# One input and one output matrix per group in the S5 scan of a decoder layer, on one core

## The chip, the cores and the metric

The kernel runs on one core of a Trainium2 chip. A core has TensorE (PE, matrix products into PSUM), VectorE (DVE), ScalarE (ACT), GpSimd (POOL) and SyncE (SP, which here issues most DMA transfers); each works through its own instructions in order and waits on semaphores for the others. The metric is the device time of one execution in microseconds (us); lower is better. The time before is the median of three executions.

## The reference

The program is one decoder layer for 1024 tokens of width 1024: half a SwiGLU block, a mixing stage (native sparse attention beside an S5 diagonal state space), the other half block, a final norm. The change touches the S5 part alone:

```python
dt = exp(log_dt); mag = exp(lr * dt)
ab_re, ab_im = mag * cos(li * dt), mag * sin(li * dt)
bu = einsum('btgh,gph->btgp', u, bb)          # complex, bb = f * b; 32 groups, 16 channels, 64 states
x[t] = ab * x[t-1] + bu[t]                    # complex, as an associative scan over 1024 tokens
y = einsum('btgp,ghp->btgh', xr, c_re) - einsum('btgp,ghp->btgh', xi, c_im) + d_skip * u
y = gelu(y); s = y * sigmoid(y @ w_glu + b_glu)
```

## The kernel before

The stages follow each other: first FFN (`gate_up7`, then `down`), input projection (`project`) with the S5 units and the compression of keys and values beside it, attention, GLU and output projection, second FFN. Most matrix products are made of three products of split operands (`mm3`, L118 to L120). S5 uses plain f32 products.

**How S5 is tiled.** 1024 tokens are 128 chunks of 8. A tile has 128 partitions: 64 states, real part in partitions 0 to 63, imaginary part in 64 to 127. In a chunk the recurrence is unrolled into matrices, so that 8 x 16 inputs of a group give the chunk's contribution to the state, and the state before the chunk gives 8 x 16 outputs. Across the 128 chunks the complex factor of a step is a length, `rho`, and an angle. The kernel turns every chunk's contribution back by the angle so far (multiplication by cosines and sines), so a real scan with `rho` does the recurrence, and turns the result forth again.

**Tables.** `s5_params` (in `gate_up7`, in the first FFN) works out what depends on the parameters and keeps it in DRAM. `s5_tables` makes the matrices in batches of four groups: four batches in the first FFN's `gate_up7`, four in its `down`. Per batch there are four tables, each of three DVE operations (helper `table`, L703 to L709); two of them (the input matrices, `s5t[0]` and `s5t[1]`) are then transposed on PE (L716), copied by ACT (L718) and stored (L719), the other two (the output matrices, `s5t[2]` and `s5t[3]`) are stored as they are (L722, L735). `s5t[4]` holds the matrices inside a chunk. `s5_phases` works out cosines and sines of 128 chunks on POOL, beside `down`, and stores them as `s5t[5]` and `s5t[6]`.

**Units.** `s5_units` has eight units of four groups, each with three steps between which the projections go on: seven loads of 256 KB on SP's queue (L804); then four matmuls with the first input matrix (L809) and four with the second (L811), DVE's two multiplications by cosines and sines (L813, L814), addition (L815), a copy that spreads `rho` into `dk` (L816), the scan (L818) and two multiplications (L819, L820) into `cz` and `sz`; then for each of four groups three matmuls into one PSUM tile, inside the chunk (L824), with `cz` (L825) and with `sz` (L826), a copy by ACT (L828) and stores (L830). Tiles with `bufs=2` are double-buffered: of the seven loads the first two, and no other.

**What sets the order.** The code is one Python program that is unrolled when it is built. A framework puts each engine's instructions in an order at build time, by priority (mostly the order of the code) and by when its own estimates have an instruction ready; it adds the waits, and a tile's buffer is only given again when its last user is done. `s5_units`, `s5_tables` and `s5_phases` are generators: the surrounding stage calls the next step at fixed places (`until`, `self.step`). The tables' steps have a lower priority than the FFN around them.

Of the kernel before, what the change touches and what calls it, by code (L numbers as in the profile page):

```python
# [9 lines left out]
F32 = mybir.dt.float32  # L10
# [3 lines left out]
AF = mybir.ActivationFunctionType  # L14
OP = mybir.AluOpType
# [4 lines left out]
P = 128  # L20
# [102 lines left out]
class Kern:  # L123
# [530 lines left out]
    def s5_tables(self, pool, b0, b1, out):  # L654
# [26 lines left out]
        for g0 in range(b0 * B, b1 * B, B):  # L681
# [18 lines left out]
            def table(x, y, zr, zi, sub, n, name):  # L700
# [7 lines left out]
                TE.tensor_tensor(o[:, :, :n], o[:, :, :n], q[:, :, :n], op=OP.subtract if sub else OP.add)  # L708
                return o  # L709

            for dst, x, y, zx, zy, sub in ((0, bp, bq, rr, ri, False), (1, bp, bq, ri, rr, True)):
                o = table(x, y, zx, zy, sub, 8, "tw")
                yield
                p = self.ps.tile([P, B, P], F32, tag="tr", name="tr", bufs=2)
                for i in range(B):
                    nc.tensor.transpose(p[:, i, :], o[:, i, :8, :].rearrange("p j h -> p (j h)"), self.ident)  # L716
                gt = pool.tile([P, B, P], F32, tag="gt", name="gt", bufs=1)
                nc.scalar.activation(gt, p, AF.Copy)  # L718
                out.dma_start(self.s5t[dst][:, gs, :], gt)  # L719
                yield  # L720
            o = table(cp, cq, ar, ai, False, 9, "tw")
            out.dma_start(self.s5t[2][:, gs, :], o[:, :, 1:9, :].rearrange("p g j h -> p g (j h)"))  # L722
# [11 lines left out]
            o = table(cq, cp, ar, ai, True, 9, "tw")  # L734
            out.dma_start(self.s5t[3][:, gs, :], o[:, :, 1:9, :].rearrange("p g j h -> p g (j h)"))  # L735
# [3 lines left out]
        for j in range(8 * (b1 == 8)):  # L739
            nc.sync.dma_start(self.s5t[4][j * 16:j * 16 + 16], self.s5k[:, :, (7 - j) * 16:(7 - j) * 16 + P])  # L740
            yield

    def s5_phases(self, pool):

        CE, B, NG, L = self.nc.gpsimd, 4, 32, 4
        pw = pool.tile([P, 14 * NG], F32, name="pw")
        CE.dma_start(pw, self.s5keep[:, self.s5keep.shape[1] - 14 * NG:])
        cw, sw = (pw[:, i * 7 * NG:(i + 1) * 7 * NG].rearrange("p (k g) -> p k g", g=NG) for i in range(2))
# [21 lines left out]
        for g0 in range(0, NG, B):  # L770
# [7 lines left out]
            CE.dma_start(self.s5t[5][:, gs, :], ct)  # L778
            CE.dma_start(self.s5t[6][:, gs, :], st)
# [3 lines left out]
    def s5_units(self, pool):  # L783
        nc, v = self.nc, self.nc.vector
        B = 4
        rho = pool.tile([P, 32], F32, name="rho")
        nc.sync.dma_start(rho, self.s5rho)
        cz, sz = (pool.tile([P, B, P], F32, name=f"z{i}") for i in range(2))
        dk = pool.tile([P, B, P], F32, name="dk")
        for t in (cz, sz, dk):  # L790
            nc.gpsimd.memset(t[:, :, 0:1], 0.0)
        for un in range(8):
# [14 lines left out]
            p0, p1 = (self.ps.tile([P, B, P], F32, tag="tr", name="tr", bufs=2) for _ in range(2))  # L807
            for i in range(B):
                nc.tensor.matmul(p0[:, i, :], tb[0][:, i, :], ut[:, uo + i, :], start=True, stop=True)  # L809
            for i in range(B):  # L810
                nc.tensor.matmul(p1[:, i, :], tb[1][:, i, :], ut[:, uo + i, :], start=True, stop=True)  # L811
            a1, a2 = (pool.tile([P, B, P], F32, tag=f"sa{i}", name=f"sa{i}", bufs=1) for i in range(2))
            v.tensor_mul(a1, p0, tb[5])  # L813
            v.tensor_mul(a2, p1, tb[6])  # L814
            v.tensor_add(a1, a1, a2)  # L815
            v.tensor_copy(dk[:, :, 1:], rho[:, gs].unsqueeze(2).to_broadcast([P, B, P - 1]))  # L816
            f = lambda t: t.rearrange("p g c -> p (g c)")
            v.tensor_tensor_scan(f(a2), f(dk), f(a1), 0.0, op0=OP.mult, op1=OP.add)  # L818
            v.tensor_mul(cz[:, :, 1:], a2[:, :, :P - 1], tb[5][:, :, :P - 1])  # L819
            v.tensor_mul(sz[:, :, 1:], a2[:, :, :P - 1], tb[6][:, :, :P - 1])  # L820
# [843 lines left out]
```

## Time and profile before

| what | value |
|---|---|
| time of three executions, us | 2045.43, 2039.56, 2040.13 (median 2040.13) |
| the profiled execution, us | 2044.72, its span 2042.9 |
| mean granted TensorE clock | 0.984 |
| busy share of the span | PE 96%, DVE 66%, ACT 41%, POOL 20% |
| loads of S5 tables (L804) | 56 of 256 KB |
| S5 tables made | about 250 to 640 us |
| S5 units on PE | 781.9 to 938.4 us |

Times in the trace are microseconds from the start of the span. A row of a timeline gives start, length, engine, line, operation, output and inputs, and in brackets how long the engine had been idle and what ended that. Matmuls are pipelined: a row's length is longer than the distance from one start to the next. Lines are those of the kernel's file; the changed file has other numbers for the same code (L809 becomes L812, L824 becomes L830, L825 becomes L831).

### The profile page before, as it was taken

How to read it: one execution, taken by the hardware profiler on the slowest of the kernel's cores; microseconds unless marked ns; L12 is line 12 of the kernel's file. 1: busy time of each engine (PE TensorE's matmuls, PEld its weight loads, DVE VectorE, ACT ScalarE, POOL GpSimd, SP SyncE). 2: the span in 40 equal slices, each digit the busy share in tenths (PEclk: the TensorE clock that was granted, in tenths of full speed). 3: DMA queues.
4: the chain of work that ended last, by engine and by line, in shares of the span. 5: the costliest groups of instructions: out<-in, count | busy, mean ns of one | idle time of the engine just before them, and what ended most of it. 6: DMA issues, size and time to landing. Idle time of an engine off the chain costs nothing.

```text
span 2042.9 us, 26293 instructions
## 1 busy us (share of the span) xinstructions
PE 1951.3 (96%) x9240; PEld 1597.8 (78%) x9240; DVE 1354.2 (66%) x2610; ACT 844.6 (41%) x1609; POOL 403.2 (20%) x552
## 2 busy tenths in 40 slices
PE   6899999999999999889899998898999999999998
PEld 5678788778877888878778887776788888888886
DVE  7768866876696462375689888767765555544546
ACT  7423333342132242143788778564233333322223
POOL 1101100114881001021565663321000000000000
PEclk9999999999999999989899999898999999999999
DMA  6343333437355354652000003653442322262312
GB/s 237 124 147 109 103 94 84 124 120 260 116 182 168 101 181 142 189 167 78 1 22 12 17 16 114 201 198 127 140 130 87 93 73 82 87 217 80 122 57 104
DMA packets 149494, 240.24 MB, mean 118 GB/s; under 512 B 18352, under 2 KB 84160, under 8 KB 149232
## 3 DMA queue, kind: packets, MB, share of 16 engines
q1 hardware_dynamic: 146112, 227.74, 35.4%
q0 software_dynamic: 3248, 10.80, 1.5%
q8 instruction: 73, 1.20, 0.2%
q14 instruction: 61, 0.50, 0.1%
HBM read 172.10 MB, written 68.49 MB: 118 GB/s over the span
## 4 chain that ended last, share of the span: by engine, by line
PE 42%; DVE 4%; POOL 2%; DMA 2%; ACT 2%; issue 2%; SPq 0%; DVEq 0%; ACTq 0%; POOLq 0%
PE dn L120 4%; PE dn L119 4%; PE dn L118 4%; PE mA L118 4%; PE mA L119 4%; PE mA L120 3%; PE pt L1053 2%; PE mB L119 2%; PE mB L120 2%; PE mB L118 2%; POOL e L1031 1%; PE s L1018 1%; PE po L1045 1%; PE po L1046 1%; PE s L1019 1%
## 5 line engine op out<-in xcount | busy, mean ns | idle before, releaser
L118 PE MATMUL mA<-f,wu 128*128 128x512 f32 x584 | 231.9, 398 | 15.5 <-DVE t L357 6.5
L457 DVE SCALAR_TENSOR_TENSOR x<-dn,x 128x512 f32<-128x512 f32 x192 | 130.6, 686 | 165.1 <-PE dn L120 151.3
L119 PE MATMUL mA<-f,wu 128*128 128x512 f32 x584 | 230.1, 394 | 0.0
L120 PE MATMUL mA<-f,wu 128*128 128x512 f32 x584 | 230.0, 394 | 0.0
L307 ACT ACTIVATE wu<-wraw 128x512 fp32r<-128x512 f32 x220 | 137.5, 629 | 188.8 <-PE mA L120 74.3
L431 ACT ACTIVATE a<-ra 128x512 fp32r<-128x512 f32 (+1 forms) x96 | 57.2, 595 | 315.8 <-PE dn L119 304.1
L308 DVE TENSOR_TENSOR wu<-wraw,wu 128x512 fp32r<-128x512 f32 x220 | 150.4, 687 | 50.1 <-ACT wu L307 48.3
L118 PE MATMUL dn<-whi,a 128*128 128x512 f32 x384 | 150.7, 392 | 0.1
L120 PE MATMUL dn<-whi,a 128*128 128x512 f32 x384 | 150.2, 392 | 0.3 <-DVE a L432 0.3
L119 PE MATMUL dn<-wlo,a 128*128 128x512 f32 x384 | 150.0, 391 | 0.0
L118 PEld LDWEIGHTS mA<-f,wu 128*128 128x128 f32 x584 | 110.1, 189 | 48.0 <-DVE t L357 10.7
L1031 POOL TENSOR_TENSOR e<-e,l 128x640 f32<-128x640 f32 (+7 forms) x128 | 132.6, 1067 | 2.5
L120 PEld LDWEIGHTS mA<-f,wu 128*128 128x128 f32 x584 | 110.2, 189 | 24.4 <-issue 0.8
L119 PEld LDWEIGHTS mA<-f,wu 128*128 128x128 f32 x584 | 110.2, 189 | 23.1 <-issue 0.6
L120 PE MATMUL dn<-f,a 128*128 128x512 f32 x320 | 124.8, 392 | 1.4 <-DVE a L432 1.4
L118 PE MATMUL dn<-f,a 128*128 128x512 f32 x320 | 125.2, 391 | 0.0
L119 PE MATMUL dn<-f,a 128*128 128x512 f32 x320 | 124.8, 390 | 0.0
L1057 DVE TENSOR_TENSOR t<-pt,t 128x512 fp32r<-128x512 f32 (+1 forms) x148 | 100.3, 683 | 14.1 <-ACT t L1056 13.4
L308 DVE TENSOR_TENSOR wu<-w,wu 128x512 fp32r<-128x512 f32 x88 | 60.5, 689 | 67.7 <-ACT wu L307 67.7
L307 ACT ACTIVATE wu<-w 128x512 fp32r<-128x512 f32 x88 | 55.1, 627 | 103.8 <-PE mB L120 46.3
L1056 ACT ACTIVATE t<-pt 128x512 fp32r<-128x512 f32 (+1 forms) x148 | 86.6, 591 | 26.5 <-PE pt L1053 23.4
L1027 ACT ACTIVATE e<-e,m 128x640 f32<-128x640 f32 (+7 forms) x128 | 93.1, 729 | 7.7 <-DVE m L1021 6.9
(402 smaller groups left out, 4954.5 us busy)
## 6 DMA issues: line engine op xcount, KB each, us to landing
wraw<-w_ffn SPq DMA_DIRECT2D x146, 512.0 KB
adt<-c SPq DMA_DIRECT2D x84, 256.0 KB
ra<-adt SPq DMA_DIRECT2D x80, 256.0 KB
st<-s5t SPq DMA_DIRECT2D x56, 256.0 KB
xs<-x SPq DMA_DIRECT2D x16, 512.0 KB
x<-xs SPq DMA_DIRECT2D x16, 512.0 KB
wraw<-w_in SPq DMA_DIRECT2D x12, 512.0 KB
x<-x SPq DMA_DIRECT2D x8, 512.0 KB
```

Of the source, the lines that this page charges most:

```text
L118: nc.tensor.matmul(p, wh, xh, start=first and i == 0, stop=False, skip_group_check=more)
L119: nc.tensor.matmul(p, wh, xl, start=False, stop=False, skip_group_check=more)
L120: nc.tensor.matmul(p, wl, xh, start=False, stop=last and i == n - 1, skip_group_check=more)
L307: nc.scalar.activation(w[:, 0], s, AF.Copy)
L308: v.tensor_sub(w[:, 1], s, w[:, 0])
L431: nc.scalar.activation(h[:, :n], r[:, :n], AF.Copy)
L457: v.scalar_tensor_tensor(x[t][:, ns], p, 0.5, x[t][:, ns], op0=OP.mult, op1=OP.add)
L1027: nc.scalar.activation(es[r][:, :w], es[r][:, :w], AF.Exp, bias=m[:, r:r + 1], scale=-1.0, accum_out=l[:, r:r + 1])
L1031: nc.gpsimd.tensor_tensor(es[r][:, :w], es[r][:, :w], l[:, r:r + 1].to_broadcast([P, w]), op=OP.mult)
L1053: nc.tensor.transpose(pt[:kw, r, :], es[r][:, b * P:b * P + kw], self.ident)
L1056: nc.scalar.activation(th[:kw], f[:kw], AF.Copy)
L1057: v.tensor_sub(tl[:kw], f[:kw], th[:kw])
```

## The change

One input matrix and one output matrix per group are left. The second input matrix differs from the first in that real and imaginary rows have changed places, with a sign; the second output matrix likewise. The changed kernel takes the one product, or the one scan, and has DVE read one half of the partitions and write the other (`halves`), with sines whose sign differs between the halves: `s5_phases` multiplies the sines' powers by `sgn` (-1 in partitions 0 to 63, +1 in the others) before it starts. `cz` now takes the difference of two products, so `sz` is gone, and one matmul with one output matrix takes the place of two. `rho` is spread into `dk` by ACT rather than DVE, and all five loads are double-buffered.

```diff
-            for dst, x, y, zx, zy, sub in ((0, bp, bq, rr, ri, False), (1, bp, bq, ri, rr, True)):
-                o = table(x, y, zx, zy, sub, 8, "tw")
...
-                out.dma_start(self.s5t[dst][:, gs, :], gt)
-                yield
+            o = table(bp, bq, rr, ri, 8, "tw")
...
+            out.dma_start(self.s5t[0][:, gs, :], gt)
+            yield
...
-            o = table(cq, cp, ar, ai, True, 9, "tw")
-            out.dma_start(self.s5t[3][:, gs, :], o[:, :, 1:9, :].rearrange("p g j h -> p g (j h)"))
...
+        sgn = pool.tile([P, 1], F32, name="sgp")
+        CE.dma_start(sgn, self.s5keep[:, :1])
+        v = pw[:, 7 * NG:]
+        CE.tensor_tensor(v, v, sgn.to_broadcast([P, 7 * NG]), op=OP.mult)
...
+        halves = [(slice(i, i + 64), slice(64 - i, 128 - i)) for i in (0, 64)]
...
-            for i in range(7):
-                t = pool.tile([P, B, P], F32, tag=f"st{i}", name=f"st{i}", bufs=2 if i < 2 else 1)
+            for i in range(5):
+                t = pool.tile([P, B, P], F32, tag=f"st{i}", name=f"st{i}", bufs=2)
...
-                nc.tensor.matmul(p1[:, i, :], tb[1][:, i, :], ut[:, uo + i, :], start=True, stop=True)
+                nc.tensor.matmul(p[:, i, :], wb[:, i, :], ut[:, uo + i, :], start=True, stop=True)
...
-            v.tensor_mul(a1, p0, tb[5])
-            v.tensor_mul(a2, p1, tb[6])
+            nc.scalar.activation(dk[:, :, 1:], rho[:, gs].unsqueeze(2).to_broadcast([P, B, P - 1]), AF.Copy)
+
+            v.tensor_mul(a1, p, co)
+            for h, o in halves:
+                v.tensor_mul(a2[h], p[o], si[o])
             v.tensor_add(a1, a1, a2)
-            v.tensor_copy(dk[:, :, 1:], rho[:, gs].unsqueeze(2).to_broadcast([P, B, P - 1]))
...
-            v.tensor_mul(cz[:, :, 1:], a2[:, :, :P - 1], tb[5][:, :, :P - 1])
-            v.tensor_mul(sz[:, :, 1:], a2[:, :, :P - 1], tb[6][:, :, :P - 1])
+
+            for h, o in halves:
+                v.tensor_mul(a1[h], a2[o], si[o])
+            v.tensor_mul(a2, a2, co)
+            v.tensor_sub(cz[:, :, 1:], a2[:, :, :P - 1], a1[:, :, :P - 1])
...
-                nc.tensor.matmul(p[:, i, :], tb[4][:, i, :], ut[:, uo + i, :], start=True, stop=False)
-                nc.tensor.matmul(p[:, i, :], tb[2][:, i, :], cz[:, i, :], start=False, stop=False)
-                nc.tensor.matmul(p[:, i, :], tb[3][:, i, :], sz[:, i, :], start=False, stop=True)
+                nc.tensor.matmul(p[:, i, :], wk[:, i, :], ut[:, uo + i, :], start=True, stop=False)
+                nc.tensor.matmul(p[:, i, :], wc[:, i, :], cz[:, i, :], start=False, stop=True)
```

The order of instructions moves with it. On PE, unit 4 before, among the products of the V projection (`pv`); `st` are the loaded tables, `tr` the PSUM tile:

```order
L120 MATMUL pv<-wv_7028,hl_5988 128x280
L809 MATMUL tr<-ut,st_7111 128x128 x4
L811 MATMUL tr<-ut,st_7113 128x128 x4
L118 MATMUL pv<-wv_7028,hh_5985 128x280
...
L824 MATMUL tr<-ut,st_7119 128x128
L825 MATMUL tr<-z_6643,st_7115 128x128
L826 MATMUL tr<-z_6644,st_7117 128x128
```

There are 24 `pv` between L811 and L824. The same unit in the changed kernel:

```order
L120 MATMUL pv<-wv_6849,hl_5837 128x280
L812 MATMUL tr<-ut,st_6928 128x128 x4
L118 MATMUL pv<-wv_6849,hh_5834 128x280
...
L830 MATMUL tr<-ut,st_6932 128x128
L118 MATMUL pv<-wv_6849,hh_5834 128x280
...
L831 MATMUL tr<-z,st_6930 128x128
```

Now 24 `pv` stand between L812 and the first L830, and 26 more between that and the first product with `z`; after it L830 and L831 alternate for the other three groups.

DVE's chain in unit 4 before:

```order
L813 TENSOR_TENSOR sa_7163<-tr,st_7121 128x512
L814 TENSOR_TENSOR sa_7164<-tr,st_7123 128x512
L815 TENSOR_TENSOR sa_7163<-sa_7163,sa_7164 128x512
L818 SCALAR_TENSOR_TENSOR sa_7164<-dk,sa_7163 128x512
L819 TENSOR_TENSOR z_6643<-sa_7164,st_7121 128x4x127
L820 TENSOR_TENSOR z_6644<-sa_7164,st_7123 128x4x127
```

The same chain in the changed kernel:

```order
L816 TENSOR_TENSOR sa_6971<-tr,st_6934 128x512
L818 TENSOR_TENSOR sa_6972<-tr,st_6936 64x512 x2
L819 TENSOR_TENSOR sa_6971<-sa_6971,sa_6972 128x512
L821 SCALAR_TENSOR_TENSOR sa_6972<-dk,sa_6971 128x512
L1202 TENSOR_TENSOR v<-pv,v 128x4x64
L824 TENSOR_TENSOR sa_6971<-sa_6972,st_6936 64x512 x2
L1203 TENSOR_TENSOR gate<-pv,gbias 128x24
L825 TENSOR_TENSOR sa_6972<-sa_6972,st_6934 128x512
L826 TENSOR_TENSOR z<-sa_6972,sa_6971 128x4x127
```

It has two pairs of half-tile operations and one more operation at the end, and a pair of the V projection's steps (L1202, L1203) now stands inside it.

SP's queue before, from the loads of unit 3's last tables on (`s5t_72` to `s5t_78` are the seven tables):

```order
L804 DMA st_6955<-s5t_74 128x512
L804 DMA st_6957<-s5t_75 128x512
L804 DMA st_6959<-s5t_76 128x512
L804 DMA st_6961<-s5t_77 128x512
L804 DMA st_6963<-s5t_78 128x512
L898 DMA cx<-kcd_84 64x2x512 x2
L804 DMA st_7111<-s5t_72 128x512
L804 DMA st_7113<-s5t_73 128x512
```

SP's queue in the changed kernel, with the loads of unit 4:

```order
L806 DMA st_6928<-s5t_72 128x512
L806 DMA st_6930<-s5t_73 128x512
L806 DMA st_6932<-s5t_74 128x512
L806 DMA st_6934<-s5t_75 128x512
L806 DMA st_6936<-s5t_76 128x512
L1185 DMA kcd_83<-cs 128x1024
```

A unit's five loads now stand together, where before the single-buffered ones were issued apart from the first two.

More of the change, by code (lines that the diff above doesn't have):

```diff
@@ L698, in s5_tables, with table @@
             yield
-            def table(x, y, zr, zi, sub, n, name):
+            def table(x, y, zr, zi, n, name):
                 o = pool.tile([P, B, 9, 16], F32, tag=name, name=name, bufs=1)
@@ L707, in table @@
                 TE.tensor_tensor(q[:, :, :n], e(y), z(zi), op=OP.mult)
-                TE.tensor_tensor(o[:, :, :n], o[:, :, :n], q[:, :, :n], op=OP.subtract if sub else OP.add)
+                TE.tensor_tensor(o[:, :, :n], o[:, :, :n], q[:, :, :n], op=OP.add)
                 return o
-            for dst, x, y, zx, zy, sub in ((0, bp, bq, rr, ri, False), (1, bp, bq, ri, rr, True)):
-                o = table(x, y, zx, zy, sub, 8, "tw")
-                yield
[L714 to L718, printed above, removed]
-                out.dma_start(self.s5t[dst][:, gs, :], gt)
-                yield
-            o = table(cp, cq, ar, ai, False, 9, "tw")
-            out.dma_start(self.s5t[2][:, gs, :], o[:, :, 1:9, :].rearrange("p g j h -> p g (j h)"))
+            o = table(bp, bq, rr, ri, 8, "tw")
+            yield
+            p = self.ps.tile([P, B, P], F32, tag="tr", name="tr", bufs=2)
+            for i in range(B):
+                nc.tensor.transpose(p[:, i, :], o[:, i, :8, :].rearrange("p j h -> p (j h)"), self.ident)
+            gt = pool.tile([P, B, P], F32, tag="gt", name="gt", bufs=1)
+            nc.scalar.activation(gt, p, AF.Copy)
+            out.dma_start(self.s5t[0][:, gs, :], gt)
+            yield
+            o = table(cp, cq, ar, ai, 9, "tw")
+            out.dma_start(self.s5t[1][:, gs, :], o[:, :, 1:9, :].rearrange("p g j h -> p g (j h)"))
             yield
@@ L777, in s5_phases @@
                 yield from level(k, gs, ct, st, ct, st, q)
-            CE.dma_start(self.s5t[5][:, gs, :], ct)
-            CE.dma_start(self.s5t[6][:, gs, :], st)
+            CE.dma_start(self.s5t[3][:, gs, :], ct)
+            CE.dma_start(self.s5t[4][:, gs, :], st)
             yield
@@ L787, in s5_units @@
         nc.sync.dma_start(rho, self.s5rho)
-        cz, sz = (pool.tile([P, B, P], F32, name=f"z{i}") for i in range(2))
-        dk = pool.tile([P, B, P], F32, name="dk")
-        for t in (cz, sz, dk):
+        cz, dk = (pool.tile([P, B, P], F32, name=n) for n in ("z", "dk"))
+        halves = [(slice(i, i + 64), slice(64 - i, 128 - i)) for i in (0, 64)]
+        for t in (cz, dk):
             nc.gpsimd.memset(t[:, :, 0:1], 0.0)
@@ L1248, in run @@
             self.ad = dr.tile([NT, P, D], F32, name="ad")
-            self.s5t = [dr.tile([P, 32, P], F32, name=f"s5t{i}") for i in range(7)]
+            self.s5t = [dr.tile([P, 32, P], F32, name=f"s5t{i}") for i in range(5)]
             self.s5k = dr.tile([16, 32, 240], F32, name="s5k")
```

7 lines of the change are left out of this document (3 added, 4 removed).

## The prediction

> **What bounds the kernel now.** I read the page's engine line first, then the busy time of each stage, then who TensorE (PE) waits for, and last the timelines of the waits that matter.
>
> ```profile
> PE 1951.3 (96%) x9240; PEld 1597.8 (78%) x9240; DVE 1354.2 (66%) x2610; ACT 844.6 (41%) x1609; POOL 403.2 (20%) x552
> ...
> 250.00:650.00 400.00, 394.65 (x1755) 313.07 (x1754) 286.48 (x475) 129.13 (x208) 128.80 (x226) 1.00 0.46 142
> 650.00:780.00 130.00, 128.88 (x599) 106.43 (x598) 68.43 (x122) 43.49 (x70) 0.23 (x3) 1.00 0.41 141
> 780.00:940.00 160.00, 141.97 (x882) 127.25 (x881) 82.88 (x109) 46.19 (x63) 24.76 (x10) 0.96 0.54 167
> 940.00:2042.00 1102.00, 1062.86 (x5043) 872.93 (x5041) 722.21 (x1451) 521.77 (x1077) 221.95 (x257) 0.98 0.29 92
> ```
>
> The columns after a stretch are its length, PE, weight load, VectorE (DVE), ScalarE (ACT), GpSimd (POOL), granted clock, DMA share, GB/s. The S5 tables are made in 250 to 650 us, where PE is busy 99% of the time; the eight S5 units run in 780 to 940, where PE has 142 of 160 us and DVE 83. So PE is the bound in both stages, and in the second about 18 us are waits. These are PE's waits from 780 to 945 us, in total, times, longest:
>
> ```profile
> PE tr L825 <- DVE z L819: 7.7, 5, 2.7
> PE pc L118 <- ACT c L918: 6.0, 2, 4.0
> PE pc L120 <- DVE c L919: 2.3, 3, 1.6
> PE tr L824 <- DVE sa L813: 0.7, 1, 0.7
> PE tr L824 <- DMA st<-s5t: 0.6, 1, 0.6
> ```
>
> The units' own waits are 7.7 + 0.7 + 0.6 = 9.0 us; the `pc` rows belong to the compression that runs between units 5 and 7.
>
> **PE work removed in the units.** Each unit loses the four matmuls of L811 and the four of L826. An f32 matmul is two records here, so four make the x8 row:
>
> ```profile
> 781.95 1.06 PE L809 MATMUL tr<-ut,st 128*128 128x128 f32 x8
> 782.84 1.06 PE L811 MATMUL tr<-ut,st 128*128 128x128 f32 x8
> 783.65 0.48 PE L120 MATMUL pp<-hh,wlo 128*128 128x512 f32 x1
> ```
>
> L811 starts 0.89 after L809, so four matmuls take 0.89 us of PE. Two such groups in eight units: 16 x 0.89 = **14.2 us**.
>
> **PE work removed in the tables.** Of 64 transposes of L716, 32 go. One stands between matmuls of the down projection:
>
> ```profile
> 566.95 0.39 PE L119 MATMUL dn<-wlo,a 128*128 128x512 f32 x1
> 567.18 0.39 PE L120 MATMUL dn<-whi,a 128*128 128x512 f32 x1
> ...
> 567.44 0.47 PE L118 MATMUL dn<-f,a 128*128 128x512 f32 x1
> 567.75 0.27 PE L716 MATMUL tr<-ident,tw 128*128 128x128 f32 x1
> 567.78 0.48 PE L119 MATMUL dn<-f,a 128*128 128x512 f32 x1
> ```
>
> Two `dn` start 0.23 apart, and 0.34 with a transpose between: 0.11 each, 32 x 0.11 = **3.5 us**. The removed table arithmetic (two tables of three DVE operations in each of eight batches), copies and stores lie beside a PE that is 99% busy; they cost the end only where PE waits for them, from 560 to 665 us:
>
> ```profile
> PE tr L716 <- DVE tw L708: 2.5, 2, 2.3
> ```
>
> Half of these transposes go, so I take **1.0 us** off (bounds: nothing, or all 2.5). The multiplication by signs that is added on POOL is one operation over 224 columns before the phases; POOL then stands idle for 131 us until the units' first memset, which hides it. Without that cover it would cost some 0.5 us (224 of the 1024 columns that take POOL 2.39 us in a row below).
>
> ```profile
> 751.43 0.30 POOL L791 MEMSET z<- 128x4 f32 x2 [131.34 <-DMA xs<-x]
> ```
>
> **The longer chain on DVE.** From the matmul's result to `z`, a unit now runs, on DVE:
>
> ```profile
> 783.04 0.69 DVE L813 TENSOR_TENSOR sa<-tr,st 128x512 f32<-128x512 f32 x1 [14.90 <-PE tr L809]
> ...
> 855.90 0.69 DVE L813 TENSOR_TENSOR sa<-tr,st 128x512 f32<-128x512 f32 x1 [3.89 <-DMA st<-s5t]
> 856.61 0.69 DVE L814 TENSOR_TENSOR sa<-tr,st 128x512 f32<-128x512 f32 x1
> 857.33 0.69 DVE L815 TENSOR_TENSOR sa<-sa,sa 128x512 f32<-128x512 f32 x1
> 858.06 1.22 DVE L818 TENSOR_TENSOR_SCAN sa<-dk,sa 128x512 f32<-128x512 f32 x1
> 859.32 0.69 DVE L819 TENSOR_TENSOR z<-sa,st 128x508 f32<-128x508 f32 x1
> ...
> 860.52 0.42 DVE L1197 TENSOR_TENSOR v<-pv,v 128x256 fp32r<-128x256 f32 x1
> ...
> 860.95 0.41 DVE L816 COPY dk<-rho 128x508 f32<-128x508 f32 x1
> ```
>
> PE takes `z` at 860.06, 4.16 us after the first multiplication starts; that one starts 1.09 us after the first matmul (783.04 against 781.95). The new chain has a half-tile operation more before the scan, and after it two halves, a multiplication and a subtraction where one multiplication stood. No row has a half-tile operation with both inputs in SBUF. The nearest is L1213/L1214, which reads 64 partitions and writes the same or the other 64:
>
> ```profile
> 918.45 0.67 DVE L1213 TENSOR_TENSOR k<-pp,k 64x512 fp32r<-64x512 f32 x1
> 919.14 0.68 DVE L1214 TENSOR_TENSOR k<-pp,k 64x512 fp32r<-64x512 f32 x1
> 919.85 0.69 DVE L814 TENSOR_TENSOR sa<-tr,st 128x512 f32<-128x512 f32 x1
> ```
>
> Half the partitions cost as much as all of them: 0.70 from start to start. The bounds are 0.35 (time by partitions) and 1.4 (twice the row); I take 0.70, since the row has the same columns and crosses halves too. The chain becomes 4.16 + 4 x 0.70 = 6.97 us, 8.06 from the first matmul. That is 2.8 us more a unit, 22.5 over eight if nothing covered it. The copy to `dk` (0.41) leaves DVE for ACT, which is busy 46 of 160 us; there it waits for the scan of the unit before, which by then is long done, so nothing queues behind it.
>
> What covers it is PE's order. After the first matmuls (0.89) and a lone L830 (0.22) the changed program holds other projections: 27 `pp` in unit 1, 24 + 3 in unit 2, 24 + 26 `pv` in units 3 and 4, 24 + 24 in unit 5. A `pp` starts every 0.227 us, a `pv` every 0.13. That covers 7.2 us in units 1 and 2, 7.6 in 3 and 4, 7.35 in 5. DVE's order puts one pair of V-projection steps into the chain in 3 to 5 (0.43, from 860.52 to 860.95), so it needs 8.5 there. Waits: 0.8, 0.8, 0.9, 0.9, 1.15. Unit 7 has six half-tile operations of K in its chain (4.2 us) against 10.8 us of PE work: 1.4. Unit 8 follows it behind a weight split and two of K: 1.0. Unit 6 has some 50 matmuls of cover: 0.5. The waits belong to in-order engines: behind a waiting L831 stand the next projections, and behind these ACT's and DVE's copies of them.
>
> The lock comes on top in unit 1. There a subtraction on POOL was under way when L815, with both inputs in SBUF, began:
>
> ```profile
> 784.27 2.39 POOL L82 TENSOR_TENSOR wlo<-wraw,whi 128x1024 fp32r<-128x1024 f32 x1 [32.51 <-PE pp L120]
> ...
> 784.66 2.55 DVE L815 TENSOR_TENSOR sa<-sa,sa 128x512 f32<-128x512 f32 x1
> ```
>
> L815 ended with the POOL operation, 1.85 us late. The new addition is ready 3.2 us after the first matmul, the POOL operation ran until 4.7: 1.5 us. The Trainium skill, "SBUF — State Buffer", section "SBUF: two separate sides", calls the pair of ports that DVE and GpSimd share an exclusive lock, which a DVE operation with two SBUF inputs needs too; the row agrees. By that rule the change is more exposed, with four operations of this kind more in a unit; if each of the four lone POOL subtractions before the compression held one for its 2.39 us, the sum would be 4 x 2.39 - 1.5 = 8 us worse.
>
> The waits add up to 0.8 + 0.8 + 0.9 + 0.9 + 1.15 + 0.5 + 1.4 + 1.0 + 1.5 = 9.0 us: what they are now. **Net of waits in the units: 0**, with bounds of -9 (all covered) and +9 (twice as long).
>
> **Loads, and the compression.** All five tables of a unit are now double-buffered, so a unit's loads no longer queue on SP behind the release of the unit before. That takes the cause of the 3.89 us above, already in the 9.0. The next wait is the compression's:
>
> ```profile
> 860.06 0.68 PE L825 MATMUL tr<-z,st 128*128 128x128 f32 x2 [2.66 <-DVE z L819]
> ...
> 866.93 0.29 PE L120 MATMUL pv<-wv,hl 128*128 128x280 f32 x1
> 871.23 0.58 PE L118 MATMUL pc<-whi,c 128*127 128x256 f32 x1 [4.00 <-ACT c L918]
> ```
>
> PE stood 4.0 us between the last `pv` and the first `pc`, for a chain of two engines. In the new order unit 5's second matmuls stand in that gap, 7 x 0.22 = 1.6 us. I take **1.7 us** off (bounds: nothing, or 2.8).
>
> **Sum.** 14.2 + 3.5 + 1.0 + 0 + 1.7 = 20.4 us less. The profiled execution took 2044.72 us (span 2042.9, 1.8 around it), so 2024.3 in its terms; it stands 4.6 above the median of 2040.13, and against that the forecast is 2019.7, **2020 us**.
>
> **Rivals.**
> *A, the clock stays up.* After two of these waits PE was granted about half its clock:
>
> ```profile
> 860.00:864.00 4.00, 3.94 (x20) 3.94 (x21) 1.36 (x5) 0.00 (x0) 0.00 (x0) 0.57 0.66 208
> ...
> 868.00:872.00 4.00, 0.77 (x2) 0.50 (x2) 2.89 (x5) 2.36 (x3) 0.00 (x0) 0.81 0.76 230
> 872.00:876.00 4.00, 3.54 (x17) 3.52 (x17) 2.84 (x3) 1.43 (x2) 0.00 (x0) 0.50 0.76 165
> ```
>
> That cost 4 x 0.43 + 4 x 0.50 = 3.7 us. If unit 5's wait shrinks to 1.15 and the one before `pc` to 2.3, both dips may go: 2016. Against it: a wait of 2.66 was enough for the first dip. The Trainium skill, "TensorE: Matmul & The Clock Gate", section "What's actually happening", puts the drop at an idle window of about 3.4 us; by that rule both dips would go. The trace's 2.66 is shorter than that, so I give it less than half.
> *B, the waits double.* POOL's subtractions and V's steps fall into the chain of every unit rather than of some: 9 us more, and the table and compression terms (2.7) come to nothing: 2020 + 11.7, 2032. For it: DVE runs in order, and the cover in every unit is 0.8 to 1.4 short, so each delay reaches PE. Against: DVE is busy 83 of 160 us.
> *C, slower.* A half-tile operation with both inputs in SBUF costs twice the 0.70. Four a unit at 0.70 more are 2.8 us, and a wait of 2.8 + 1 sets off a dip like that at 860 (1.7 us): 8 x 4.5 = 36, 2056. It decides from about 1.1 us for an operation: the wait of 1 us then grows by 4 x 0.42 = 1.7 to the 2.7 that set off that dip, and 1.7 + 1.7 a unit is more than the gain, 20.4 / 8 = 2.6. Against it: L1214 crosses halves at 0.68.
> That the work doesn't fall away is no rival: the changed order has no second L809 group and no third matmul.
>
> **Numbers.** Forecast 0.64 (own range 2012 to 2028), A 0.17, B 0.14, C 0.05. What this kernel can tell from no change is 0.3%, 6 us: under 2034.0 is faster. Forecast and A are, and half of B: 0.64 + 0.17 + 0.07 = 0.88; the rest of B is no change, 0.08; C less a rest that ends there, 0.04. The range must hold the forecast, most of A and half of B: 2007 to 2033.
>
> **What would show it.** PE's records fall by 128 + 32; L812 starts with 0.89 us to the next matmul. The half-tile rows of L818 and L824 read 0.68 to 0.70; 1.2 or more speaks for C. PE's wait for `z` at L831 totals about 9 us in eight pieces around 1 us; 18 speaks for B. The row of 4 us before `pc` reads about 2, and the clock from 845 to 870 tells A. The units' last matmul now starts at
>
> ```profile
> L826 PE MATMUL tr<-z,st x64: 275/275/421, 790.0 to 938.4; 128*128 128x128 f32 x64
> ```
>
> 156.5 us after the first one at 781.95. That stretch is some 16 shorter (14.2 + 1.7), and everything from 940 on keeps its length; if that grows, the forecast is wrong in what it leaves out.

## The result and the profile after

| what | before | after |
|---|---|---|
| median of four executions each, us | 2042.78 | 2011.79 |
| lowest and highest, us | 2039.56, 2049.48 | 2007.87, 2016.59 |
| the profiled execution, us (its span) | 2044.72 (2042.9) | 2011.34 (2009.5) |

The ratio is 0.9837, with a 95% interval of 0.9819 to 0.9855: 31 us less by the medians, where the prediction had 20. The engine line of the page after, and the stages in the columns of the prediction's first fence:

```profile
PE 1926.0 (96%) x9080; PEld 1576.6 (78%) x9080; DVE 1332.2 (66%) x2578; ACT 844.9 (42%) x1609; POOL 399.3 (20%) x545
```

```profile
250.00:650.00 400.00, 397.03 (x1759) 317.70 (x1758) 258.92 (x433) 126.16 (x202) 121.73 (x220) 1.00 0.45 139
...
770.00:915.00 145.00, 131.90 (x783) 115.91 (x782) 95.10 (x127) 51.50 (x71) 28.02 (x14) 0.96 0.49 154
```

PE's records fall by 160, the 128 + 32 that were forecast, and PE is still the bound of both stages. To place the gain, the two traces are read at marks that both programs have: one operation of VectorE in the first FFN's `gate_up7`, the first matmul of the down projection (`dn`), the first and the last of the projections (`pp`). Before, a row of VectorE's timeline, then two groups of the view of line L118 (count, min/median/max ns, first and last start):

```profile
289.14 0.69 DVE L362 TENSOR_TENSOR c<-mB,t 128x512 f32<-128x512 f32 x1
```

```profile
L118 PE MATMUL dn<-f,a x320: 387/389/502, 472.0 to 1990.5; 128*128 128x512 f32 x160
L118 PE MATMUL pp<-hh,whi x192: 389/389/503, 742.7 to 976.0; 128*128 128x512 f32 x192
```

After, the same two views:

```profile
288.65 0.69 DVE L362 TENSOR_TENSOR c<-mB,t 128x512 f32<-128x512 f32 x1
```

```profile
L118 PE MATMUL dn<-f,a x320: 387/389/502, 468.7 to 1957.5; 128*128 128x512 f32 x160
L118 PE MATMUL pp<-hh,whi x192: 389/389/502, 733.1 to 945.1; 128*128 128x512 f32 x192
```

| stretch, us | before | before, again | after | after, again | change |
|---|---|---|---|---|---|
| mark to first `dn` (tables 0 to 3) | 182.9 | 182.8 | 180.1 | 180.0 | -2.8 |
| first `dn` to first `pp` (tables 4 to 7) | 270.7 | 270.9 | 264.4 | 265.7 | -5.8 |
| first to last `pp` (units, compression) | 233.3 | 232.5 | 212.0 | 212.0 | -20.9 |

The columns "again" are a second profile of each kernel, from the experiments. Together -29.5, which is the 31 within what the medians scatter. The last `pp` to the last `dn` is 1058.0 and 1056.0 us before, 1055.9 and 1059.2 after: no change. The prediction's own measure of the units, from their first matmul to their last, fell from 156.5 to 139.4, 17.1 less where it had some 16; but 261 `pp` now lie inside it instead of 241, so the projections as a whole are compared here. So 8.6 us came from the tables, where the prediction had 3.5 + 1.0 = 4.5, and 20.9 from the projections with the units, where it had 14.2 + 0 + 1.7 = 15.9.

PE's waits in the units, after (770 to 945 us, in total, times, longest):

```profile
PE tr L831 <- DVE z L826: 6.3, 7, 1.3
PE pc L118 <- ACT c L923: 4.1, 2, 2.4
PE pc L120 <- DVE c L924: 2.1, 2, 1.3
```

They were 7.7 + 0.7 + 0.6 = 9.0 for the units and 6.0 and 2.3 for the compression. Unit by unit, on PE's timeline (units 1, 4 and 5, two waits of the compression, units 7 and 8; units 2 and 3 waited 0.73 and 0.97, unit 6 not at all):

```profile
781.24 0.46 PE L831 MATMUL tr<-z,st 128*128 128x128 f32 x2 [1.00 <-DVE z L826]
...
829.42 0.49 PE L831 MATMUL tr<-z,st 128*128 128x128 f32 x2 [0.76 <-DVE z L826]
842.39 0.49 PE L831 MATMUL tr<-z,st 128*128 128x128 f32 x2 [1.02 <-DVE z L826]
845.90 0.38 PE L118 MATMUL pc<-whi,c 128*127 128x256 f32 x1 [1.68 <-ACT c L923]
856.89 0.58 PE L118 MATMUL pc<-whi,c 128*127 128x256 f32 x1 [2.41 <-ACT c L923]
901.12 0.49 PE L831 MATMUL tr<-z,st 128*128 128x128 f32 x2 [1.25 <-DVE z L826]
910.73 0.49 PE L831 MATMUL tr<-z,st 128*128 128x128 f32 x2 [0.61 <-DVE z L826]
```

The forecast for them was 2.3 (with the lock), 0.8, 0.9, 0.9, 1.15, 0.5 (unit 6), 1.4, 1.0. The chain that makes them, in unit 4 on DVE:

```profile
822.04 0.69 DVE L816 TENSOR_TENSOR sa<-tr,st 128x512 f32<-128x512 f32 x1
822.74 1.39 DVE L818 TENSOR_TENSOR sa<-tr,st 64x512 f32<-64x512 f32 x2
...
826.03 0.40 DVE L1202 TENSOR_TENSOR v<-pv,v 128x256 fp32r<-128x256 f32 x1
...
828.68 0.69 DVE L826 TENSOR_TENSOR z<-sa,sa 128x508 f32<-128x508 f32 x1
```

Two half-tile operations take 1.39 us, and from the first row to the last one's end it is 7.33 us; the prediction had 6.97 + 0.43 for the step of the V projection between them.

### The profile page after: what moved, and what is told of

Same layout as the page of the kernel before. It is cut to its first block, busy times and chain, and to the rows that moved or that the text cites. A ratio compares the mean times of both kernels' runs of the same rounds, so it can differ in the third digit from the quotient of the medians.

```text
span 2009.5 us, 25871 instructions
## 1 busy us (share of the span) xinstructions
PE 1926.0 (96%) x9080; PEld 1576.6 (78%) x9080; DVE 1332.2 (66%) x2578; ACT 844.9 (42%) x1609; POOL 399.3 (20%) x545
## 3 DMA queue, kind: packets, MB, share of 16 engines
q8 instruction: 71, 1.16, 0.2%
## 4 chain that ended last, share of the span: by engine, by line
PE 51%; DVE 9%; DMA 3%; ACT 3%; POOL 2%; issue 2%; SPq 0%; DVEq 0%; ACTq 0%; POOLq 0%
PE dn L120 6%; PE dn L119 6%; PE dn L118 6%; PE mA L118 4%; PE mA L119 3%; PE mA L120 3%; PE pt L1058 2%; DMA wraw<-w_ffn 2%; PE mB L119 1%; PE mB L120 1%; PE mB L118 1%; PE po L1050 1%; PE pp L120 1%; PE s L1023 1%; PE pp L119 1%
## 5 line engine op out<-in xcount | busy, mean ns | idle before, releaser
L118 PE MATMUL mA<-f,wu 128*128 128x512 f32 x584 | 232.1, 399 | 17.1 <-DVE t L357 7.4
L118 PE MATMUL dn<-whi,a 128*128 128x512 f32 x384 | 150.5, 392 | 0.0
L118 PEld LDWEIGHTS mA<-f,wu 128*128 128x128 f32 x584 | 110.5, 189 | 48.9 <-DVE t L357 11.6
L118 PE MATMUL dn<-f,a 128*128 128x512 f32 x320 | 124.9, 390 | 0.0
```

Source lines behind the costliest of these rows:

```text
L118: nc.tensor.matmul(p, wh, xh, start=first and i == 0, stop=False, skip_group_check=more)
```

## The experiments

Twelve kernels ran, in three groups of four, each group with runs of the kernel before on the same chip (medians of that kernel 2048.4, 2048.0 and 2047.8). Medians are therefore compared by their ratio to the kernel before, and single stages by the marks above.

**The same kernels again.**

> The changed kernel once more, as a measure of how far two profiles of one kernel differ. If the stage lengths are a property of the program, the first projection matmul again starts at 733 us, the unit matmuls last 139.5 us from first to last, each within 0.7 us, and the waits for z at L831 total 6.3 within 0.7. If they vary from run to run by as much as the whole time does (2007.9 to 2016.6), nothing can be read from differences of a few us between single profiles.

> The kernel before once more, for its stage lengths. If they are a property of the program, the stretch from the first to the last projection matmul is again 233.7 us within 0.7, the stretch from the first matmul of the down projection to the first of the projections again 270.7 within 1.5, and the unit waits for z 7.7. The stretch before it, from the first matmul of the gate and up products, was 402.2 here against 395.3 to 401.1 in five profiles of changed kernels; if the change shortened it, it is again above 401.5, and if that stretch only varies, it falls among them.

Measured: ratios 0.9835 [0.9813, 0.9856] and 0.9996 [0.9977, 1.0015]. The stretches stand in the table above, and the waits for `z` were 6.3 again, before 7.3. The three stretches of the table repeat to 0.8 us (1.3 in `down`). What lies ahead of them and behind them repeats less: over all profiles the mark at L362 lay between 285.0 and 290.9, and from the last `pp` to the last `dn` the two profiles of the changed kernel differ by 3.3. The expectation's 402.2 us were 402.1 again, above those of the changed kernels (395.3 to 401.1), so by its own reading the change shortens that stretch. It begins ahead of the mark, though, and from the mark on the change shortens it by 2.8; whether any more of it is the change's is not shown.

**The removed matmuls back.** Each group of the input matrix and each matmul inside the chunk is issued twice on the same data.

```diff
-            for i in range(B):
-                nc.tensor.matmul(p[:, i, :], wb[:, i, :], ut[:, uo + i, :], start=True, stop=True)
+            for i in range(2 * B):
+                nc.tensor.matmul(p[:, i % B, :], wb[:, i % B, :], ut[:, uo + i % B, :], start=True, stop=True)
...
+                nc.tensor.matmul(p[:, i, :], wk[:, i, :], ut[:, uo + i, :], start=True, stop=True)
                 nc.tensor.matmul(p[:, i, :], wk[:, i, :], ut[:, uo + i, :], start=True, stop=False)
```

> The changed kernel with the removed matmul records put back: the L812 group and each matmul of L830 are issued twice on the same data. By the prediction's term, 16 x 0.89, the stretch from the first to the last projection matmul grows from 212.4 by 14.2. If the matmuls were partly hidden behind the waits for z (6.3 us in seven), the second L830 ahead of the wait covers 0.22 of each, and it grows by some 12.7. If much of the 21.3 us gained in that stretch came from the loads and the clock instead of the matmuls, it grows by less than 10.

Measured: the projections take 227.0 instead of 212.0 (first to last L118 of `pp`), 15.0 more; the waits for `z` are 5.5 instead of 6.3, and one wait of 1.0 in the compression is new. Ratio 0.9897 [0.9871, 0.9923], against 0.9835 for the changed kernel. The 14.2 of the prediction holds to within a us or two (this kernel also has 3.41 us more at half the clock): matmuls that were removed in front of a PE that is the bound came off one for one. The other 6 us of this stage are something else.

**One buffer for four of the five tables.**

```diff
-                t = pool.tile([P, B, P], F32, tag=f"st{i}", name=f"st{i}", bufs=2)
+                t = pool.tile([P, B, P], F32, tag=f"st{i}", name=f"st{i}", bufs=2 if i < 1 else 1)
```

> The changed kernel with one buffer instead of two for four of the five loaded tables of a unit. If double buffering carries part of the gain in the units (no wait for st, no dip of the clock at 860), the unit stretch grows from 139.5 by 3 to 6 us, with a wait for st in the list of waits and a dip behind it. If the shorter load list (five instead of seven) is what ended the wait, it stays within 1 us.

Measured: the units take 149.7 from first to last matmul, 10.2 more, and the projections 221.3, 9.3 more. In the whole time less of it shows (ratio 0.9851 [0.9828, 0.9873], median 2018.61 against 2015.91 on the same chip; the profiled execution was the longest of its four, 2023.44), so 9.3 is what it cost in that execution, and its mean may be less. Unit 5 on the timelines of DVE and PE, then the window of 4 us behind it:

```profile
845.07 1.39 DVE L818 TENSOR_TENSOR sa<-tr,st 64x512 f32<-64x512 f32 x2 [4.00 <-DMA st<-s5t]
...
852.02 0.80 PE L831 MATMUL tr<-z,st 128*128 128x128 f32 x2 [5.29 <-DVE z L826]
```

```profile
852.00:856.00 4.00, 3.80 (x16) 3.53 (x16) 2.89 (x3) 1.59 (x2) 0.00 (x0) 0.54 0.45 141
```

DVE waits 4.00 us for the sines, PE 5.29 for `z`, and the clock is at 0.54 behind it. It is the same place, and the same 4 us, as the 3.89 in the kernel before. Five loads instead of seven do not end this wait; the second buffer does. And with the longer chain the late load costs PE 5.29 where it cost 2.66: without the second buffer the change would have lost here part of what it wins. Not all of the 9.3 is the loads', though. In unit 1 PE waits 2.76 for `z` instead of 1.00, and half the clock follows for 3.41 us (worth up to 1.7); there DVE waited for no load, but its addition stood beside a subtraction of GpSimd:

```profile
776.28 2.40 POOL L82 TENSOR_TENSOR wlo<-wraw,whi 128x1024 fp32r<-128x1024 f32 x1 [32.86 <-ACT whi L81]
776.57 2.66 DVE L819 TENSOR_TENSOR sa<-sa,sa 128x512 f32<-128x512 f32 x1
```

That leaves some 6 us for the loads and the dips behind them.

**The table stage, put back whole and in parts.** First the two tables with transposes, copies and stores; then only their arithmetic; then only the transposes.

```diff
+            o = table(bp, bq, rr, ri, 8, "tw")
+            yield
...
+                nc.tensor.transpose(p[:, i, :], o[:, i, :8, :].rearrange("p j h -> p (j h)"), self.ident)
...
+            out.dma_start(self.s5t[5][:, gs, :], gt)
...
+            o = table(cp, cq, ar, ai, 9, "tw")
+            out.dma_start(self.s5t[6][:, gs, :], o[:, :, 1:9, :].rearrange("p g j h -> p g (j h)"))
```

> The changed kernel with the table stage of before put back: two more tables a batch, the 32 transposes, the copies and the stores, into DRAM tiles that nothing reads. The units stay as changed. If the gain of 9.6 us ahead of the first projection is all table work, that matmul starts at 742 to 743 instead of 733.1 and the time grows by 9 to 10. By the prediction's two table terms it grows by 4.5. If a good part is something else that the change moved (the order of the down projection, the phases), it grows by less than 3. The units keep their 139.5.

The arithmetic alone:

```diff
             o = table(bp, bq, rr, ri, 8, "tw")
             yield
+            o = table(bp, bq, rr, ri, 8, "tw")
+            yield
...
+            table(cp, cq, ar, ai, 9, "tw")
```

> The changed kernel with only the DVE arithmetic of the two removed tables done again (48 operations), without their transposes, copies and stores. By the prediction the arithmetic was worth 1.0 us through PE's waits (bounds 0 and 2.5): first projection matmul at 734. If the mis-sized part is DVE's load, which makes PE wait for the inputs of the down projection and for tables, 5 to 6 us come back: 738 to 739.

The transposes alone:

```diff
-            for i in range(B):
-                nc.tensor.transpose(p[:, i, :], o[:, i, :8, :].rearrange("p j h -> p (j h)"), self.ident)
+            for i in range(2 * B):
+                nc.tensor.transpose(p[:, i % B, :], o[:, i % B, :8, :].rearrange("p j h -> p (j h)"), self.ident)
```

> The changed kernel with its 32 transposes of the tables issued twice, the second time over the first. By the prediction, 32 x 0.11 = 3.5 us more from the first matmul of the down projection to the first of the projections (some of the 32 lie before it). If the arithmetic on VectorE is the whole of the table stage's gain, under 1 us, since the doubled arithmetic alone gave back 5.9 at the first projection matmul and the whole stage 6.2.

| kernel | mark to first `dn`, us | first `dn` to first `pp`, us | PE's waits in the second, us | ratio to before |
|---|---|---|---|---|
| before | 182.9 | 270.7 | 5.4 | 1 |
| after (and again) | 180.1 (180.0) | 264.4 (265.7) | 2.6 (3.5) | 0.9835 [0.9813, 0.9856] |
| stage put back | 182.8 | 268.5 | 3.9 | 0.9868 [0.9846, 0.9890] |
| arithmetic alone | 178.9 | 273.5 | 11.0 | 0.9862 [0.9841, 0.9884] |
| transposes alone | 181.9 | 269.7 | 5.7 | 0.9864 [0.9832, 0.9896] |

The waits of PE in the down projection, before, then after, then with the arithmetic alone:

```profile
PE tr L716 <- DVE tw L708: 2.5, 2, 2.3
PE dn L120 <- DVE a L432: 1.7, 4, 0.9
PE tr L726 <- DVE tw L708: 1.2, 2, 0.7
```

```profile
PE dn L120 <- DVE a L432: 1.2, 2, 0.9
PE tr L725 <- DVE tw L708: 0.7, 1, 0.7
PE tr L715 <- DVE tw L708: 0.7, 1, 0.7
```

```profile
PE dn L120 <- DVE a L432: 5.7, 5, 1.6
PE tr L717 <- DVE tw L708: 2.3, 1, 2.3
PE dn L118 <- ACT a L431: 1.5, 1, 1.5
PE tr L727 <- DVE tw L708: 1.5, 2, 0.8
```

In `gate_up7` the parts behave as the prediction thought: there 16 transposes are worth 1.8 us (181.9 against 180.1), 0.11 each, and arithmetic costs nothing (178.9, even 1.2 less). In `down` they do not: the arithmetic alone gives back 9.1, of which 8.4 are waits, the transposes alone 5.3 (1.8 by the 0.11, 3.1 waits), both together with copies and stores 4.1, all against 264.4 (six other profiles with the changed table stage gave 264.1 to 265.7). Over both stretches that is 7.9, 7.1 and 6.8: the two parts add up to 15.0, over twice what the whole stage returns. So there is no price of the arithmetic or of a transpose to be had here. Each version is another order of steps, and each leaves PE other waits for the split `a`, which DVE computes in its order among the tables. The stage put back also stays 2.2 short of before in `down`; which of its small differences in order that is was not settled.

**What makes DVE late in `down`.** There GpSimd computes the phases; in `gate_up7` it computes nothing. DVE's first multiplication of the input table, before, in the first and in the second of these stages (eight of each; busy us, mean ns of one):

```profile
L706 DVE TENSOR_TENSOR tw<-b,kt 128x512 f32<-128x512 f32 x8 | 5.5, 684 | 0.0
...
L706 DVE TENSOR_TENSOR tw<-b,kt 128x512 f32<-128x512 f32 x8 | 7.3, 915 | 1.8 <-PE tr L716 1.8
```

So two kernels computed the phases of the first four groups only and stored them eight times: the changed one, and the one with the arithmetic put back.

```diff
-            for k in range(L, 7):
-                yield from level(k, gs, ct, st, ct, st, q)
+            for k in range(L, 7):
+                if g0 == 0:
+                    yield from level(k, gs, ct, st, ct, st, q)
+                else:
+                    yield
+                    yield
```

> The changed kernel without seven eighths of the phases: GpSimd computes the cosines and sines of the first four groups only and stores these eight times, with the same steps and transfers, so the outputs are not the reference's. For comparison with the next kernel. If GpSimd's operations stretch VectorE's (a table operation took 0.68 before the down projection, where GpSimd computes nothing, and 0.81 to 0.96 in it), L706 to L708 read 0.68 to 0.76 throughout, PE's waits in the down projection (2.9 us) fall under 1, and the stretch from its first matmul to the first projection matmul falls from 264.4 to about 262.

> The kernel that does the arithmetic of the two removed tables again, likewise without seven eighths of the phases, so the outputs are not the reference's. With the phases this arithmetic made the down projection's stretch 273.5 instead of 264.4 and PE's waits in it 11.0 instead of 2.9. If the arithmetic costs PE time only where GpSimd stretches VectorE, the stretch comes within 1.5 us of the kernel without phases above (about 263). If it is VectorE's load itself, or the place of the steps, it stays 5 or more above it.

Measured from first `dn` to first `pp`: 262.0 and 268.0 (with the phases 264.4 and 273.5); ratios 0.9815 [0.9792, 0.9837] and 0.9840 [0.9820, 0.9859]. The changed kernel without phases has 0.9 us of waits in that stretch, as expected (2.6 with the phases, where the expectation has 2.9); its two multiplications of the input table still take 0.79 and 0.94 in the mean, beside the phases that are left, and the other table operations are in the range that was expected. With the arithmetic put back and no phases, the operation in `down`, and PE's waits there, read

```profile
L706 DVE TENSOR_TENSOR tw<-b,kt 128x512 f32<-128x512 f32 x8 | 5.8, 728 | 0.0
```

```profile
PE dn L120 <- DVE a L432: 3.2, 3, 1.6
PE dn L118 <- ACT a L431: 1.5, 1, 1.5
```

The operation is back at 0.73, and the waits for tables are gone, but the arithmetic still costs 6.0 of its 9.1 us, 3.8 of it in waits for `a` that remain (4.7, the two rows, against 0.9). So GpSimd's stretching is roughly a third of the effect (each number is one profile's, and this stretch varies by 1.6 among profiles of the changed table stage). The rest is DVE's own load or the place of the steps, which no run here separates, so the expectation of "within 1.5 us" fell. The Trainium skill, "SBUF — State Buffer", section "SBUF: two separate sides", has a GpSimd operation that reads SBUF and a DVE operation with two SBUF inputs exclude each other; the means fit that (684 alone, 915 beside GpSimd), and the additions of the units show it directly (below, in the part on the hardware).

**What the exchange of halves costs.** Each pair of half-tile operations is replaced by one over the full tile, which leaves out the exchange of real and imaginary rows.

```diff
-            for h, o in halves:
-                v.tensor_mul(a2[h], p[o], si[o])
+            v.tensor_mul(a2, p, si)
...
-            for h, o in halves:
-                v.tensor_mul(a1[h], a2[o], si[o])
+            v.tensor_mul(a1, a2, si)
```

> The changed kernel with each pair of half-tile operations replaced by one operation over all 128 partitions, which leaves out the exchange of real and imaginary rows, so the outputs are not the reference's. The chain on VectorE is 2 x 0.69 = 1.4 us shorter in a unit. If the waits for z (6.3 us in seven, longest 1.25) are the chain's overhang over PE's cover, they go to about 0 and the stretch from the first to the last projection matmul falls from 212.4 by 5 to 6. If a part of each wait is something else (a lock of the ports, the copies of the V projection in VectorE's order), more than 2 us of waits stay.

Measured: the projections take 213.2 (729.4 to 942.6), 1.2 more than with the exchange, at a ratio of 0.9817 [0.9802, 0.9833]. PE's waits there:

```profile
PE pc L118 <- ACT c L921: 6.5, 2, 4.0
PE tr L829 <- DVE z L824: 5.9, 6, 1.4
```

A chain 1.4 us shorter in each of eight units leaves the waits for `z` at 5.9. The reason stands in PE's order: the framework, whose estimate of `z` is now earlier too, puts the second matmuls earlier. Between the first and the second group stand 22 `pp` instead of 27 in unit 1, 24 instead of 27 in unit 2, 24 + 16 `pv` instead of 24 + 26 in units 3 and 4; and in unit 5 they end ahead of the last seven `pv`, so that the gap before `pc` is empty again and 4.0 long. Neither theory had this. The overhang holds for a given order; but the framework chooses the cover anew for every chain, and comes out up to 1.4 us short. The second theory has a part in it too: in units 1 and 3 the addition, which now starts earlier beside GpSimd's subtraction, took 1.63 us instead of 0.84 and 0.83, so there only 0.6 of the 1.4 was won.

**A later second half.** If the framework comes out short by 1 us, a lower priority for the second matmuls should mend it. In a first version all four L831 have it; in a second one unit 5 has all eight matmuls behind the last `pv`, in the gap before the compression.

```diff
             for i in range(B):
-                nc.tensor.matmul(p[:, i, :], wk[:, i, :], ut[:, uo + i, :], start=True, stop=False)
-                nc.tensor.matmul(p[:, i, :], wc[:, i, :], cz[:, i, :], start=False, stop=True)
+                nc.tensor.matmul(p[:, i, :], wk[:, i, :], ut[:, uo + i, :], start=i == 0, stop=False)
+            with self.tc.high_priority(offset=-40):
+                for i in range(B):
+                    nc.tensor.matmul(p[:, i, :], wc[:, i, :], cz[:, i, :], start=False, stop=i == B - 1)
```

> A version that is meant to be shorter: the four matmuls of L830 stand together, and the four of L831 behind them with a priority that is 40 lower, so that 3 to 9 more projections lie ahead of the wait for z in units 1 to 6. If the 6.3 us of waits are only missing cover, they fall to about 2.5 and the time by 3 to 4 us. If a later second half only moves the wait to the output's copies or to the next unit, the stretch from the first to the last projection matmul keeps its 212.4.

In the second version the first loop of unit 5 (`un == 4`) has the offset of -40 too.

> The version with the later second halves, with unit 5 set apart: there all eight matmuls stand behind the last matmul of the V projection, in the gap before the compression. In the version before it the waits for z fell from 6.3 to 2.6, but the wait before the first pc grew from 1.68 to 3.36, with the clock at half after it, and the stretch from the first to the last projection matmul was 211.1 instead of 212.4. If that gap is what took the gain, the wait is again under 2.3, no dip follows it, and the stretch is 208 to 209.5. If the gap is the longer by what is put in it, it stays at 211.

Measured: first version, waits for `z` 2.6, but 3.36 before the first `pc`, and the projections take 210.6 by L118, 1.4 less than 212.0 (in the expectation's count, which ends with the last matmul of any line, 211.1 instead of 212.4); ratio 0.9821 [0.9793, 0.9849], so the 3 to 4 us that were expected of the time did not show. Second version: 209.2 by L118 (733.7 to 942.9), 2.8 less than 212.0, and 209.7 in the expectation's count, just above its range. Its waits, and the stretch at half the clock behind the first `pc`:

```profile
PE pc L118 <- ACT c L926: 4.7, 2, 2.4
PE tr L834 <- DVE z L826: 3.2, 5, 1.7
PE pc L120 <- DVE c L927: 2.4, 2, 1.6
```

```profile
844.41:847.83 3.42, 3.27 (x15) 3.28 (x16) 2.26 (x3) 1.19 (x2) 0.00 (x0) 0.50 0.56 146
```

The wait before the first `pc` is 2.27, as expected, but a dip follows it all the same: 3.41 us at half the clock, as long as in the changed kernel's first profile (846.66 to 850.07), where the first version has twice that (845.27 to 852.10). The ratio is 0.9807 [0.9790, 0.9825], the lowest of all kernels here (median 2009.64, against 2047.81 for the kernel before). The 2.8 us are read from the stage in one profile; in the whole time the interval overlaps that of the changed kernel, so a gain there is not shown.

## Why the prediction was right, and where its sizes were off

*The matmuls, 14.2.* Right: 15.0 came back with them. In the changed trace the first group is followed 0.89 later by the next matmul, as was said:

```profile
772.84 1.06 PE L812 MATMUL tr<-ut,st 128*128 128x128 f32 x8
773.73 0.39 PE L830 MATMUL tr<-ut,st 128*128 128x128 f32 x2
```

*The tables, 3.5 + 1.0.* This is the step that failed, by size: "The removed table arithmetic ... lie beside a PE that is 99% busy; they cost the end only where PE waits for them", and of these waits half, 1.0. The two stretches with tables lost 8.6. The transposes' 0.11 is confirmed in `gate_up7` (1.8 for 16), so the 3.5 may stand; the remaining 5 are several times the 1.0 and beyond its bound of 2.5. Two things were left out. The arithmetic is also waited for through `a`, which DVE computes among the tables (1.7 in the waits of before, 5.7 with the arithmetic alone, 0.9 of it in either case one wait that the changed kernel has too). The prediction didn't read that row, nor the 1.2 of L726, because it asked only who waits for the tables that go. And a share of 99% over 400 us says nothing of the 50 us in which DVE, of whose time 72% was taken over the whole stretch, had no gap left (before, in the columns of the stages):

```profile
550.00:600.00 50.00, 48.23 (x214) 35.72 (x213) 48.69 (x78) 15.45 (x25) 43.89 (x67) 1.00 0.52 162
```

Waits explain 1.9 to 2.8 us of the 5 (5.4 before, 2.6 and 3.5 after); the rest is open, and no run here prices it.

*Waits in the units, net 0.* 9.0 were forecast and 6.3 came, so 2.7 less. By unit the forecast was off by 0.07 to 0.15 in units 2 to 5 and 7 and by 0.4 to 0.5 in 6 and 8, where it was too high. The lock's 1.5 in unit 1 did not happen:

```profile
773.94 2.40 POOL L82 TENSOR_TENSOR wlo<-wraw,whi 128x1024 fp32r<-128x1024 f32 x1 [31.94 <-PE tr L812]
...
776.06 0.84 DVE L819 TENSOR_TENSOR sa<-sa,sa 128x512 f32<-128x512 f32 x1
```

GpSimd's subtraction ended 3.5 us after the first matmul of 772.84 rather than 4.7, and the addition lost 0.15 (0.84 instead of 0.69). That is luck of the order: the subtraction began 1.10 after the first matmul, where it had been 2.32 before, and in the kernel with one buffer, where it was 3.0, the addition took 2.66. Two readings of the prediction are wrong here. The addition of before did not end with the subtraction but 0.55 behind it (787.21 against 786.66). And a unit has two operations with two SBUF inputs more, not four: the addition, the scan, the halves of L824, L825 and L826, against L815, L818, L819 and L820. The other waits came from the right mechanism, an overhang over the cover that the prediction had counted in the changed order; the run without the exchange shows that it can't be carried over to another chain, since the cover moves with it.

*Loads and compression, 1.7.* The direction was right: 4.00 before `pc` became 1.68, though the second such wait grew from 2.0 to 2.4; together 1.9, and 0.2 from the row below it. In the second profiles of both kernels the two rows fell from 8.3 to 7.6 only. The prediction priced the second buffer at the wait it removes. Taking it away cost 9.3 in the profiled execution, at most some 6 of it through the loads.

*Rival A* came in part, and how much of it is chance. Before, the clock was at half three times, from 860.22, 870.46 and 884.12 on, for 13.65 us in all; the prediction showed the first two, and priced the windows around them at 3.7. After, it was at half from 846.66 and from 856.90 on, for 10.24 us: the dip behind unit 5's wait is gone, and the one before `pc` is not. But in the second profile of the changed kernel, whose waits at this place are the same (1.02, 1.68, 0.76), it was at half for 3.41 us only, from 859.79 on. The place of the waits in a grid of 3.41 us differs. In the first profile 1.94 us of PE's idle time fell into one stretch of the grid, and the next one is at half; in the second 1.58 and 1.16 fell into two, and none is:

```profile
843.25:846.66 3.41, 1.47 (x11) 1.07 (x9) 2.21 (x3) 1.76 (x3) 0.00 (x0) 1.00 1.02 275
846.66:850.07 3.41, 2.91 (x13) 2.92 (x14) 2.52 (x2) 0.82 (x1) 0.00 (x0) 0.50 0.52 139
```

```profile
842.72:846.13 3.41, 1.83 (x14) 1.64 (x14) 2.60 (x5) 2.56 (x4) 0.00 (x0) 1.00 1.05 320
846.13:849.55 3.42, 2.26 (x17) 2.05 (x17) 3.00 (x2) 0.35 (x1) 0.00 (x0) 1.00 0.77 176
```

Nor is a dip here worth half its length. Of the seven profiles whose units are those of the changed kernel (both of its own, and those that differ in the tables or the phases alone), three had 10.24 us at half and took 212.0, 212.5 and 212.1 us for the projections; four had 3.41 and took 212.0, 211.7, 211.6 and 211.6. So 6.83 us at half, 3.4 by the prediction's way of pricing, are worth some 0.5: around the compression PE waits for ACT and DVE, and what the clock does not take, these waits take (6.2 us in the first profile, 7.6 in the second). Of the projections' 20.9, 14.2 are the matmuls and 2.1 to 2.7 the units' waits; the other 4 lie in the compression's waits and the clock, and don't divide between them.

*Rival B* is refuted by the 6.3, *C* by the half-tile rows, all 32 of which lie close to a full tile's time:

```profile
L818 DVE TENSOR_TENSOR sa<-tr,st x16: 683/688/693, 774.6 to 905.1; 64x512 f32<-64x512 f32 x16
L824 DVE TENSOR_TENSOR sa<-sa,st x16: 684/686/690, 778.3 to 908.5; 64x512 f32<-64x512 f32 x16
```

*Everything from 940 on keeps its length*: so it is.

The time was in the range, at the forecast's own lower edge (2011.8 against 2012). The sign and the largest term were right for the reason given; the 10 us that were missing lie 4 in the tables, 5 in waits and clock of the projections, and the rest in the scatter.

## What to carry to other kernels

Work taken off the engine that is the bound can be priced by the distance between two starts, and it came off one for one; work taken off its supplier cannot be read from "who waits for it", since whatever is queued behind it on the supplier is late as well, above all in the stretches where that engine has no gap. Where a build-time order is made from estimates, a shorter or longer chain moves the cover with it: look at how much the framework puts in between, and try to shift that, before shortening the chain. A chain that grows makes the loads ahead of it dearer (5.29 us for a late load of 4.00, where it had been 2.66 for 3.89), so buffer them twice in the same change. And a dip of the clock is priced by what the stretch takes with it and without it, in several profiles, not by its length.

## What the runs showed of the hardware that was not expected

- Half the clock was granted for whole stretches of a grid of 3.41 us: four, three and one of them in the projections above (13.65, 10.24 and 3.41 us). A window of 4 us like that from 860 to 864 in the prediction reads 0.57 because 3.41 us of it are at 0.50. From 750 to 950 us, in all fourteen profiles, a stretch at full clock was followed by one at half whenever PE had been idle for 1.77 us or more of it, and never when it had been 1.73 or less. Behind 950 us PE's idle time alone doesn't decide it: the clock was halved after as little as 1.03 and not after 1.86. The Trainium skill, "TensorE: Matmul & The Clock Gate", section "What's actually happening", puts the drop at an idle window of about 3.4 us; the length of the window agrees, but here about half of one, idle, was enough.
- A DVE operation with two SBUF inputs over 128 x 512 took 684 ns on average where GpSimd was idle, and 915 where GpSimd computed phases beside it. The units' additions show how: one that began while GpSimd's subtraction ran ended 0.55 us behind the subtraction, whether that made it 0.84 us long (after), 1.63 (without the exchange), 2.55 (before) or 2.66 (with one buffer).
- DVE reads one half of the partitions and writes the other, with both inputs in SBUF, at 686 ns for 64 x 512, the time of a full tile: with the same 512 columns, half the partitions cost as much as all.
